# Last expert's down weights in four pieces by output columns, each added and normed as it comes; the final gain spread by TensorE

## The chip, the cores and the metric

The kernel runs on one core of one Trainium2 chip. The metric is the device time of one execution in microseconds (us). A core has TensorE (PE, matmuls, with its weight loads shown apart as PEld), VectorE (DVE), ScalarE (ACT), GpSimd (POOL) and SyncE (SP, which here issues nearly all DMAs). On-chip data lie in SBUF; matmul results lie in PSUM, which has eight banks of 128 partitions x 512 fp32 values.

## The reference

One decoder block on 256 tokens of width 1024, all in fp32: two attentions merged by gates, a residual, a hierarchical mixture of 32 experts, a second residual, and a last RMSNorm. What matters here is the end:

```python
def hier_moe(h, ...):
    ...                      # gates: (tokens, 32), two experts of one group per token
    out = jnp.zeros_like(hf)
    for e in range(N_EXPERTS):
        a = jax.nn.silu(hf @ w_e_gate[e]) * (hf @ w_e_up[e])     # 1024 -> 512
        out = out + gates[:, e:e + 1].astype(hf.dtype) * (a @ w_e_down[e])   # 512 -> 1024
    return out.reshape(b, t, d)
...
    x = x + hier_moe(rmsnorm(x, g_ffn[l]), ...)
return rmsnorm(x, g_final)
```

The last norm divides each token's row by the root of the mean of its squares and multiplies it by `g_final`, column by column.

## The kernel before

The 256 tokens are two tiles of 128 (NT = 2). The first 300 us, called the front here, are projections, the two attentions, the output projection and the routing; PE works nearly without a break there. Then comes the loop over 32 experts. Every expert has up to 32 slots (CAP) for its tokens. Its weights come in six chunks of 1 MB, four of gate/up and two of down, into a ring of 24 slots of SBUF, issued by SP in the order of use, with eight DMAs outstanding.

For each expert, `gateup` makes the activations (`gu`), `finish` transposes them (`atp`, copied to SBUF by DVE in L938) and multiplies them by the down weights. Here the width of 1024 is cut in four groups of 256 columns (REP = 4), and the four groups' matmuls fill four bands of 32 partitions of one bank `dn`. ACT and DVE then scale by the gate and split the result into a high and a low part, `y_hi` (L951) and `y_lo` (L953). `scatter_matrix` has made `ct`, a 0/1 matrix that spreads slots to tokens, and 16 matmuls per expert add both parts to the running sums, which stay in four PSUM banks `quad0` to `quad3` for the whole loop. Bank g holds columns 256g to 256g + 255 for both token tiles; the view is `yacc[g][:, t, :]`. The residual is added in the same banks. In the front the same four banks serve as work space: for transposes at the start, for the scores of the attentions (two banks per step, in turn) and for the router.

Small matmuls without use (`idle`, made by `busy`) stand between the chunks of the last two experts. The last expert's second down chunk comes in two DMAs of 512 KB, so that its last eight matmuls need only the last half. In the last expert the 16 matmuls into the banks go bank by bank. Behind it `norm` (L970 to L984) works through the sums, first token tile, then second: for each bank ACT squares it with a running sum (`zq`, L974), DVE multiplies it by the gain (`zo`, L975); then a reduce, a root (L271), a reciprocal (L272), a scaling of half the columns by each of ACT (L981) and DVE (L983), and two DMAs of 256 KB (L984). The gain `gf`, `g_final` broadcast to all partitions, comes by a DMA of 512 KB (L1086) behind the last weights, into a slot of the ring; `zq` and `zo` take two more slots. `general`, which follows, holds work for the case that an expert gets more tokens than slots; it is a branch that isn't taken.

Within an engine, instructions run in the order of the program. Waits between engines are semaphores, set from the tiles: an instruction waits for what touched its tile last on another engine. Two engines that read one PSUM tile also go one after the other: DVE's product on a bank waits for ACT's square on it.

Of the kernel before, what the change touches and what calls it, by code (L numbers as in the profile page):

```python
# [9 lines left out]
F32 = mybir.dt.float32  # L10
# [3 lines left out]
AF = mybir.ActivationFunctionType  # L14
ALU = mybir.AluOpType
AX = mybir.AxisListType

P = 128
T = 256
D = 1024  # L20
NT = T // P
NK = D // P
EPS = 1e-6
NE = 32
NG = 4
HID = 512
CAP = 32
REP = P // CAP
# [56 lines left out]
def tile_hybrid_block(  # L85
    ctx: ExitStack,
    tc: tile.TileContext,
    x, g_mix, w_in, w_kvs, sinks, w_br_dil, w_br_swa, w_out, g_ffn, w_group, b_group,
    w_router, b_router, w_e_gu, w_e_down, g_final, c_small, c_big, out,
):  # L90
    nc = tc.nc
    x, out = x[0], out[0]
# [7 lines left out]
    def slot(i, shape, name, dt=F32):  # L100
        return sb.tile(shape, dt, tag=f"s{i}", name=name)

    quad = [ps.tile([P, 512], F32, tag=f"quad{g}", name=f"quad{g}") for g in range(4)]

    def bank(tag, shape, name):
        return ps.tile(shape, F32, tag=tag, name=name)
# [537 lines left out]
    chunks = {}  # L644
    nchunk = [0]

    def fill(t, e, what, i):
        if what == 0:
            SP.dma_start(t, w_e_gu[e, i].rearrange("p u r c -> p (u r c)"))
        else:  # L650
            parts = 2 if (e, i) == (NE - 1, 1) else 1
            n = 2 // parts
            for j in range(parts):
                SP.dma_start(
                    t[:, 1024 * n * j:1024 * n * (j + 1)],
                    w_e_down[e, i, :, n * j:n * (j + 1), :].rearrange("p c o -> p (c o)"))

    def next_slot(name):
        nchunk[0] += 1
        return slot(ring[(nchunk[0] - 1) % len(ring)], [P, 2048], name)  # L660
# [272 lines left out]
    def finish(e):  # L933
# [28 lines left out]
               e == 0 and t == 0 and i == 0, e == NE - 1 and i == 1)  # L962
        yield

    cts = {}


# [3 lines left out]
    def norm(gf, zq, zo):  # L971
        for t in range(NT):
            for g in range(REP):
                A.activation(zq, yacc[g][:, t, :], AF.Square, accum_out=fs[:, t, g:g + 1])  # L974
                V.tensor_tensor(out=zo[:, t, g, :], in0=yacc[g][:, t, :], in1=gf[:, g, :], op=ALU.mult)  # L975
            V.tensor_reduce(fr[:, t:t + 1], fs[:, t, :], axis=AX.X, op=ALU.add)
            rstd_of(fr[:, t:t + 1], fr[:, t:t + 1])
            for h in range(2):
                z = zo[:, t, 2 * h:2 * h + 2, :]
                if h == 1:  # L980
                    A.activation(z, z, AF.Copy, scale=fr[:, t:t + 1])  # L981
                else:
                    V.tensor_scalar(z, z, fr[:, t:t + 1], None, op0=ALU.mult)  # L983
                SP.dma_start(out[t * P:(t + 1) * P, 512 * h:512 * h + 512], z.rearrange("p g c -> p (g c)"))  # L984

    def general(*tiles):

# [72 lines left out]
    for e in range(NE):  # L1060
# [14 lines left out]
        if e == NE - 1:  # L1075
            busy(e, 2)
        prefetch(4)
        fin = finish(e)
        cts[e] = scatter_matrix(e)
        run(fin)  # L1080
        run(gat)
        run(fin)
        prefetch(2)
        if e == NE - 2:
            gf = next_slot("gf")
            SP.dma_start(gf[:, 0:D], g_final.rearrange("(a d) -> a d", a=1).to_broadcast([P, D]))  # L1086
    run(fin)
    ordered[0] = False
    zq = next_slot("zq")[:, 0:256]
    zo = next_slot("zo").rearrange("p (t g c) -> p t g c", t=NT, g=REP)  # L1090
    tiles = (gf[:, 0:D].rearrange("p (g c) -> p g c", g=REP), zq, zo)
    norm(*tiles)
    general(*tiles)


_INS = ["x", "g_mix", "w_in", "w_kvs", "sinks", "w_br_dil", "w_br_swa", "w_out", "g_ffn", "w_group", "b_group",
        "w_router", "b_router", "w_e_gu", "w_e_down", "g_final"]


def _blocks(w):  # L1100
# [5 lines left out]
def _laid_out(inputs):  # L1106
# [8 lines left out]
        a[name] = _blocks(a[name][0])  # L1115
    gu = np.stack([a["w_e_gate"][0], a["w_e_up"][0]], axis=1)
    a["w_e_gu"] = gu.reshape(NE, 2, 4, 2, P, HID).transpose(0, 2, 4, 1, 3, 5)
    a["w_e_down"] = a["w_e_down"][0].reshape(NE, 2, 2, P, D).transpose(0, 1, 3, 2, 4)
    return a

# [26 lines left out]
```

## Time and profile before

| | |
|---|---|
| time, median of 3 runs | 750.15 us (749.88 to 750.56) |
| profiled execution | 749.57 us |
| its span, first to last instruction | 747.8 us |
| mean granted TensorE clock | 0.922 of full speed |
| busy: PE, DVE, ACT | 644.3, 297.0, 224.5 us |
| DMA, whole span | 249.87 MB, 334 GB/s |

Times in the rows are microseconds from the start of the span. A busy share is the share of a stretch in which an engine had an instruction in work; the chain of work is followed back from the last instruction, at each step to what released it. The granted clock is given as a share of 2.4 GHz, so that 0.50 is 1.2 GHz.

### The profile page before, as it was taken

The numbers are of one execution on the slowest core, as the hardware profiler recorded it, in microseconds if no ns is written. First come the engines' busy times: TensorE is split into PE (matmuls) and PEld (weight loads), VectorE is DVE, ScalarE is ACT, GpSimd is POOL, SyncE is SP. The second block draws the span as 40 slices with busy tenths as digits, with TensorE's granted clock in tenths as the row PEclk, the third lists the DMA queues.
The fourth block names the chain that finished last, engine by engine and source line by source line (L and its number), as shares of the span: only waits on it lengthen the run. The fifth ranks groups of instructions, "written<-read, shape, count | busy, mean of one in ns | idle before, by whom it ended". The sixth has DMA issues, their size and how long they took to land.

```text
span 747.8 us, 14858 instructions
## 1 busy us (share of the span) xinstructions
PE 644.3 (86%) x6416; PEld 459.5 (61%) x6416; DVE 297.0 (40%) x753; ACT 224.5 (30%) x448; POOL 2.1 (0%) x10
## 2 busy tenths in 40 slices
PE   9999999999999999999987687887678778777783
PEld 8999988888998998655544344344334434433341
DVE  6554767985788566532222112112111211111103
ACT  6444566775888443211101000001000000000004
POOL 0000000000000000000000000000000000000000
PEclk9999999999999999999999979789887978977887
DMA  8756446338837978999999999999999999999993
GB/s 323 270 188 223 142 142 223 114 114 293 327 114 293 348 272 288 369 388 419 419 418 420 419 420 420 419 419 422 420 419 422 418 420 421 420 420 420 420 417 123
DMA packets 39333, 249.87 MB, mean 334 GB/s; under 512 B 6608, under 2 KB 8032, under 8 KB 9824
## 3 DMA queue, kind: packets, MB, share of 16 engines
q1 hardware_dynamic: 39104, 248.81, 83.5%
q8 instruction: 52, 0.85, 0.5%
q10 hardware_dynamic: 160, 0.07, 0.1%
q14 instruction: 17, 0.14, 0.0%
HBM read 247.82 MB, written 1.05 MB: 333 GB/s over the span
## 4 chain that ended last, share of the span: by engine, by line
DMA 51%; PE 35%; DVE 7%; ACT 5%; issue 1%; SPq 0%; DVEq 0%; ACTq 0%
DMA ew<-in_w_e_gu_dram 30%; PE acc L119 23%; DMA ew<-in_w_e_down_dram 21%; PE gu L119 3%; DVE wh L244 3%; PE quad L119 2%; PE dn L119 1%; ACT wh L243 1%; ACT pps L500 1%; PE ga L119 1%; PE spun L119 1%; PE dpv L119 1%; PE dtp L580 1%; DVE kal L406 1%; DVE qs L396 1%
## 5 line engine op out<-in xcount | busy, mean ns | idle before, releaser
L119 PE MATMUL gu<-ew,xes 128*32 128x256 f32 x2048 | 153.7, 418 | 28.7 <-DMA ew<-in_w_e_gu_dram 28.5
L119 PE MATMUL acc<-hT_hi,wh 128*128 128x256 f32 x800 | 145.2, 283 | 0.8 <-DVE qa L396 0.8
L119 PEld LDWEIGHTS acc<-hT_hi,wh 128*128 128x128 f32 x800 | 121.6, 188 | 2.6 <-DVE qa L396 1.0
L119 PEld LDWEIGHTS gu<-ew,xes 128*32 128x32 f32 x2048 | 62.7, 117 | 88.6 <-DMA ew<-in_w_e_gu_dram 43.3
L244 DVE TENSOR_TENSOR wh<-w,wh 128x1024 fp32r<-128x1024 f32 (+1 forms) x84 | 100.2, 1198 | 35.0 <-ACT wh L243 33.1
L119 PE MATMUL acc<-hT_lo,wh 128*128 128x256 f32 x400 | 111.3, 279 | 0.0
L243 ACT CAST wh<-w 128x1024 fp32r<-128x1024 f32 (+1 forms) x84 | 86.2, 1028 | 41.4 <-PE acc L119 40.3
L119 PE MATMUL dn<-ew,ws 128*32 128x256 f32 x1024 | 82.9, 457 | 5.0 <-DMA ew<-in_w_e_down_dram 4.2
L925 DVE TENSOR_TENSOR ws<-ws,gu 128x128 f32<-128x128 f32 x32 | 9.2, 286 | 184.5 <-ACT ws L922 184.5
L119 PEld LDWEIGHTS acc<-hT_lo,wh 128*128 128x128 f32 x400 | 75.1, 188 | 0.0
L922 ACT ACTIVATE ws<-gu 128x128 f32<-128x128 f32 x32 | 8.9, 278 | 205.9 <-PE gu L119 205.9
L119 PEld LDWEIGHTS dn<-ew,ws 128*32 128x32 f32 x1024 | 32.2, 125 | 34.4 <-issue 10.7
L951 ACT ACTIVATE y_hi<-dn,gsl 128x256 fp32r<-128x256 f32 x32 | 15.2, 474 | 113.6 <-PE dn L119 113.6
L953 DVE SCALAR_TENSOR_TENSOR y_lo<-dn,gsl,y_hi 128x256 fp32r<-128x256 f32 x32 | 15.5, 484 | 67.9 <-ACT y_hi L951 67.9
L119 PE MATMUL ga<-ws,x_again 128*128 128x128 f32 x256 | 37.5, 307 | 4.8 <-DVE ws L938 3.8
L119 PEld LDWEIGHTS ga<-ws,x_again 128*128 128x128 f32 x256 | 34.2, 215 | 8.7 <-DVE ws L938 6.7
L119 PE MATMUL quad<-y_hi,cts 32*128 32x256 f32 x256 | 23.7, 355 | 15.0 <-ACT y_hi L951 15.0
L860 ACT ACTIVATE xes<-ga,fcol 128x128 f32<-128x128 f32 x32 | 11.6, 367 | 77.1 <-DVE xes L862 77.1
L119 PEld LDWEIGHTS quad<-y_hi,cts 32*128 32x128 f32 x256 | 13.9, 204 | 33.1 <-ACT y_hi L951 31.8
L119 PE MATMUL quad<-y_lo,cts 32*128 32x256 f32 x256 | 32.1, 386 | 2.4
L892 DVE TENSOR_SCALAR ws<-cs,pos 128x128 f32<-128x128 f32 x64 | 17.9, 282 | 40.4 <-PE ct L119 40.4
L119 PEld LDWEIGHTS quad<-y_lo,cts 32*128 32x128 f32 x256 | 18.6, 201 | 21.6 <-issue 13.9
(199 smaller groups left out, 737.0 us busy)
## 6 DMA issues: line engine op xcount, KB each, us to landing
ew<-in_w_e_gu_dram SPq DMA_DIRECT2D x128, 1024.0 KB, 19.8
ew<-in_w_e_down_dram SPq DMA_DIRECT2D x63, 1024.0 KB, 20.0
w<-in_w_in_dram SPq DMA_DIRECT2D x29, 1024.0 KB, 5.1
w<-in_w_br_swa_dram SPq DMA_DIRECT2D x4, 1024.0 KB, 5.3
w<-in_w_out_dram SPq DMA_DIRECT2D x4, 1024.0 KB, 5.1
w<-in_w_br_dil_dram SPq DMA_DIRECT2D x2, 1024.0 KB, 4.8
xt<-in_x_dram SPq DMA_DIRECT2D x2, 512.0 KB, 4.4
w<-in_w_in_dram SPq DMA_DIRECT2D x2, 512.0 KB, 6.4
```

The lines of the kernel that those rows point to most:

```text
L119: i = PE.matmul(o, lhsT, rhs, start=start, stop=stop, skip_group_check=True)
L243: order(A.copy(w[:, 0, :, :ncol], r))
L244: order(V.tensor_tensor(out=w[:, 1, :, :ncol], in0=r, in1=w[:, 0, :, :ncol].bitcast(F32), op=ALU.subtract))
L396: V.scalar_tensor_tensor(out=lo, in0=sv, scalar=cs[own, j:j + 1], in1=hi.bitcast(F32), op0=ALU.mult, op1=ALU.subtract)
L406: V.tensor_tensor(out=kal[r, b, c, :], in0=ov[own], in1=ka[own, b, c, :].bitcast(F32), op=ALU.subtract)
L500: A.activation(v, v, AF.Exp, bias=nm[:, i:i + 1], scale=-1.0, accum_out=den[:, i:i + 1])
L860: A.activation(dst, src, AF.Copy, scale=col)
L892: eq = V.tensor_scalar(dd[:, t, :].rearrange("p (g s) -> p g s", g=REP), cs[:, C_CNT:C_CNT + CAP].unsqueeze(1).to_broadcast([P, REP, CAP]) ...
L922: A.activation(ac, gu[:, 0:P], AF.Silu)
L925: V.tensor_tensor(out=ac, in0=ac, in1=gu[:, P:2 * P], op=ALU.mult)
L951: A.activation(y_hi, dn[:, 0:256], AF.Copy, scale=gsl)
L953: V.scalar_tensor_tensor(out=y_lo, in0=dn[:, 0:256], scalar=gsl, in1=y_hi.bitcast(F32), op0=ALU.mult, op1=ALU.subtract)
```

## The change

The four banks become one PSUM tile of four banks, `quads`, with `quad[g]` as views of it and a view `acc4` by token tile. The host lays out the last expert's down weights a second time, `w_e_last`, as four pieces; piece g holds, of each of the four groups of 256 columns, the columns 64g to 64g + 63, for all 512 inputs. They come in four DMAs of 512 KB in place of one of 1 MB and two of 512 KB.

The last expert has its own `finish_last`. For each piece in turn it does 16 down matmuls of 64 columns into a bank of its own, one scaling by the gate on DVE (`y`, plain fp32, no split), 8 plain fp32 matmuls that add 64 columns to each bank for both token tiles, and two squares on ACT, each over 64 columns in all four banks of one token tile. The products by the gain for piece g (`gained`) are written behind the `y` of piece g + 1. `norm_rest` then does the reduce, root and reciprocal once for both token tiles, the scalings (ACT 512 and 256 columns, DVE 512 and 768) and four output DMAs.

`g_final` comes as 4 KB in eight rows on ACT's queue at expert 2; at expert 29 `gains` spreads it over the partitions by eight matmuls and ACT copies it into the slot `gf`. The slots for `gf` and `zo` are taken at expert 28.

```diff
-    quad = [ps.tile([P, 512], F32, tag=f"quad{g}", name=f"quad{g}") for g in range(4)]
+    quads = ps.tile([P, 4, 512], F32, tag="quad", name="quad")
+    quad = [quads[:, g, :] for g in range(4)]
+    acc4 = quads.rearrange("p g (t c) -> p g t c", t=NT)
...
-            parts = 2 if (e, i) == (NE - 1, 1) else 1
-            n = 2 // parts
-            for j in range(parts):
-                SP.dma_start(
-                    t[:, 1024 * n * j:1024 * n * (j + 1)],
-                    w_e_down[e, i, :, n * j:n * (j + 1), :].rearrange("p c o -> p (c o)"))
+            if e == NE - 1:
+                for j in range(2):
+                    SP.dma_start(t[:, 1024 * j:1024 * j + 1024], w_e_last[2 * i + j].rearrange("p c j o -> p (c j o)"))
+            else:
+                SP.dma_start(t, w_e_down[e, i].rearrange("p c o -> p (c o)"))
...
+    def finish_last(e):
...
+        ct, gsl = cts.pop(e)
+        for g in range(REP):
+            dn = bank(("V", f"A{1 - e % 2}", "T", f"A{e % 2}")[g], [P, 512], f"dn{e}_{g}")
+            w = chunks[(e, 1, g // 2)][:, 1024 * (g % 2):1024 * (g % 2) + 1024].rearrange("p (c j o) -> p c j o", c=4, j=REP)
+            for c in range(4):
+                for j in range(REP):
+                    mm(dn[CAP * j:CAP * j + CAP, 0:64], aT[:, CAP * c:CAP * c + CAP], w[:, c, j, :], c == 0, c == 3)
+            y = sb.tile([P, 64], F32, tag=("yh", "yl")[g % 2], name=f"y{e}_{g}")
+            pin(V.tensor_scalar(y, dn[:, 0:64], gsl, None, op0=ALU.mult))
+            if g:
+                gained(g - 1)
+            for t in range(NT):
+                for j in range(REP):
+                    r = slice(CAP * j, CAP * j + CAP)
+                    mm(yacc[j][:, t, 64 * g:64 * g + 64], ct[r, t * P:(t + 1) * P].bitcast(F32), y[r, :], False, True)
+            for t in range(NT):
+                pin(A.activation(end["tiles"][1].rearrange("p (g c) -> p g c", g=REP), quarter(t, g), AF.Square,
+                                 accum_out=fs[:, t, g:g + 1]))
+        gained(REP - 1)
+        norm_rest()
...
+    def quarter(t, g):
+        return acc4[:, :, t, 64 * g:64 * g + 64]
+
+    def gained(g):
+        gf, zq, zo = end["tiles"]
+        for t in range(NT):
+            c = slice(64 * g, 64 * g + 64)
+            pin(V.tensor_tensor(out=zo[:, t, :, c], in0=quarter(t, g), in1=gf[:, :, c], op=ALU.mult))
+
+    def norm_rest():
+        gf, zq, zo = end["tiles"]
+        pin(V.tensor_reduce(fr, fs, axis=AX.X, op=ALU.add))
+        pin(A.activation(fr, fr, AF.Sqrt, scale=1.0 / D, bias=eps))
+        pin(V.reciprocal(fr, fr))
+        for t, k in ((0, 2), (1, 1)):
+            z = zo[:, t, 0:k, :]
+            pin(A.activation(z, z, AF.Copy, scale=fr[:, t:t + 1]))
+            SP.dma_start(out[t * P:(t + 1) * P, 0:256 * k], z.rearrange("p g c -> p (g c)"))
+            z = zo[:, t, k:, :]
+            pin(V.tensor_scalar(z, z, fr[:, t:t + 1], None, op0=ALU.mult))
+            SP.dma_start(out[t * P:(t + 1) * P, 256 * k:D], z.rearrange("p g c -> p (g c)"))
+
+    def gains():
...
+            for k in range(4):
+                mm(o[:, k * P:(k + 1) * P], ident[0:8, 4 * h + k:4 * h + k + 1].to_broadcast([8, P]), grows, True, True)
+            A.copy(gf[:, 2 * h:2 * h + 2, :], o.rearrange("p (g c) -> p g c", g=2))
...
-        if e == NE - 2:
+        if e == 2:
+            A.dma_start(grows, g_final.rearrange("(k p) -> k p", p=P))
+        if e == NE - 3:
+            gains()
+        if e == NE - 4:
             gf = next_slot("gf")
-            SP.dma_start(gf[:, 0:D], g_final.rearrange("(a d) -> a d", a=1).to_broadcast([P, D]))
+            zo = next_slot("zo").rearrange("p (t g c) -> p t g c", t=NT, g=REP)
```

On PE, the last expert before, from the transpose of its activations on (`atp`); `dn` are the down matmuls, `ew` the weight slots, `ws` the activations, `quad_61` to `quad_64` the four banks:

```order
L125 MATMUL atp_6646<-cs,ws 128x128
L119 MATMUL idle_6649<-y_hi_6562 128x256 x2
L119 MATMUL dn_6652<-ew_6291,ws 32x256 x8
L119 MATMUL dn_6652<-ew_6293,ws 32x256 x8
L119 MATMUL quad_61<-y_hi_6669,cts_6642 128x256 x2
L119 MATMUL quad_61<-y_lo_6670,cts_6642 128x256 x2
...
L119 MATMUL quad_64<-y_hi_6669,cts_6642 128x256 x2
L119 MATMUL quad_64<-y_lo_6670,cts_6642 128x256 x2
```

And the same place on PE after the change:

```order
L127 MATMUL atp_6657<-cs,ws 128x128
L121 MATMUL idle_6660<-y_hi_6575 128x256 x2
L121 MATMUL dn_0_6663<-ew_6289,ws 32x64 x16
L121 MATMUL quad<-y_0_6680,cts_6653 128x64 x8
L121 MATMUL dn_1_6692<-ew_6289,ws 32x64 x16
L121 MATMUL quad<-y_1_6709,cts_6653 128x64 x8
L121 MATMUL dn_2_6723<-ew_6292,ws 32x64 x16
L121 MATMUL quad<-y_2_6740,cts_6653 128x64 x8
L121 MATMUL dn_3_6754<-ew_6292,ws 32x64 x16
L121 MATMUL quad<-y_3_6771,cts_6653 128x64 x8
```

One round of 16 down matmuls and 16 adds has become four rounds of 16 narrow down matmuls and 8 narrow adds, with the down of a piece behind the add of the one before.

On DVE, from the copy of the transposed activations to the end, before:

```order
L938 COPY ws<-atp_6646 128x128
L953 SCALAR_TENSOR_TENSOR y_lo_6670<-dn_6652,gsl_6643,y_hi_6669 128x256
L975 TENSOR_TENSOR zo<-quad_61,gf 128x256
L975 TENSOR_TENSOR zo<-quad_62,gf 128x256
L975 TENSOR_TENSOR zo<-quad_63,gf 128x256
L975 TENSOR_TENSOR zo<-quad_64,gf 128x256
L976 TENSOR_REDUCE fr<-fs 128x1
...
L975 TENSOR_TENSOR zo<-quad_64,gf 128x256
L976 TENSOR_REDUCE fr<-fs 128x1
L272 RECIPROCAL fr<-fr 128x1
L983 TENSOR_SCALAR zo<-zo,fr 128x512
```

And after:

```order
L972 COPY ws<-atp_6657 128x128
L983 TENSOR_SCALAR y_0_6680<-dn_0_6663,gsl_6654 128x64
L983 TENSOR_SCALAR y_1_6709<-dn_1_6692,gsl_6654 128x64
L1026 TENSOR_TENSOR zo<-quad,gf 128x4x64 x2
L983 TENSOR_SCALAR y_2_6740<-dn_2_6723,gsl_6654 128x64
L1026 TENSOR_TENSOR zo<-quad,gf 128x4x64 x2
L983 TENSOR_SCALAR y_3_6771<-dn_3_6754,gsl_6654 128x64
L1026 TENSOR_TENSOR zo<-quad,gf 128x4x64 x4
L1030 TENSOR_REDUCE fr<-fs 128x2
L1032 RECIPROCAL fr<-fr 128x2
L1038 TENSOR_SCALAR zo<-zo,fr 128x512
L1038 TENSOR_SCALAR zo<-zo,fr 128x768
```

The products of a piece stand behind the `y` of the next one, each `L1026` reads all four banks, and the two norms, one for each token tile, have become one. On ACT the eight squares now stand in a row, ahead of one root and two scalings.

## Rows read from the trace of the kernel before

**Rows 1.** The cores view: span and mean granted clock.

```profile
core 0: 747.8 us, clock 0.922
```

**Rows 2.** The page: its chain's shares by engine, and its costliest group.

```profile
DMA 51%; PE 35%; DVE 7%; ACT 5%; issue 1%; SPq 0%; DVEq 0%; ACTq 0%
L119 PE MATMUL gu<-ew,xes 128*32 128x256 f32 x2048 | 153.7, 418 | 28.7 <-DMA ew<-in_w_e_gu_dram 28.5
```

**Rows 3.** Stretches: PE, PEld, DVE, ACT, POOL busy (instructions), granted clock, DMA share, GB/s.

```profile
700.00:723.30 23.30, 18.72 (x191) 9.14 (x186) 3.10 (x10) 1.50 (x4) 0.00 (x0) 0.78 1.01 420
723.30:727.00 3.70, 3.27 (x49) 1.79 (x38) 0.00 (x0) 0.00 (x0) 0.00 (x0) 1.00 1.01 415
...
734.60:737.00 2.40, 1.76 (x24) 1.02 (x24) 0.48 (x1) 0.57 (x2) 0.00 (x0) 0.98 0.06 24
737.00:743.00 6.00, 0.24 (x5) 0.00 (x0) 4.54 (x14) 5.40 (x20) 0.00 (x0) 0.50 0.15 51
```

**Rows 4.** Timeline, last expert: start, duration, engine, line, operation [idle before <-releaser].

```profile
732.18 0.62 PEld L119 LDWEIGHTS dn<-ew,ws 128*32 128x32 f32 x16 [0.41 <-DVE ws L938]
732.21 1.79 PE L119 MATMUL dn<-ew,ws 128*32 128x256 f32 x24 [0.23 <-DVE ws L938]
...
733.36 0.16 PEld L119 LDWEIGHTS dn<-ew,ws 128*32 128x32 f32 x8 [0.56 <-DMA ew<-in_w_e_down_dram]
734.62 0.64 PE L119 MATMUL dn<-ew,ws 128*32 128x256 f32 x8 [0.62 <-DMA ew<-in_w_e_down_dram]
```

**Rows 5.** The same timeline, the norm.

```profile
736.91 0.38 ACT L974 ACTIVATE zq<-quad 128x256 f32<-128x256 f32 x1 [1.11 <-PE quad L119]
...
737.41 0.38 ACT L974 ACTIVATE zq<-quad 128x256 f32<-128x256 f32 x1
737.41 1.95 DVE L975 TENSOR_TENSOR zo<-quad,gf 128x256 f32<-128x256 f32 x4 [1.10 <-ACT zq L974]
...
741.23 0.42 DVE L975 TENSOR_TENSOR zo<-quad,gf 128x256 f32<-128x256 f32 x1
...
741.56 0.15 DVE L976 TENSOR_REDUCE fr<-fs 128x1 f32<-128x4 f32 x1
...
742.27 0.49 DVE L983 TENSOR_SCALAR zo<-zo,fr 128x512 f32<-128x512 f32 x1
```

**Rows 6.** Tile gf (min/median/max ns, first and last start), then the output's line.

```profile
L975 DVE TENSOR_TENSOR zo<-quad,gf x8: 418/425/425, 737.4 to 741.2; 128x256 f32<-128x256 f32 x8
...
DMA to landing us min/median/max: 16.1/16.1/16.1
...
L984 SPq DMA_DIRECT2D out_dram<-zo x4: 332/379/678, 741.3 to 743.2; - x4
```

**Rows 7.** Timeline and clocks of narrow matmuls: eight, four and four, then sixteen.

```profile
297.92 1.08 PE L119 MATMUL quad<-wr,ws 128*128 128x36 f32 x8 [0.30 <-DVE ws L703]
...
702.21 0.50 PE L119 MATMUL ct<-gate,ws 128*128 128x1 f32 x4
...
717.55 0.85 PE L119 MATMUL ct<-gate,ws 128*128 128x1 f32 x4
...
702.00:703.00 1.00, 1.00 (x13) 0.81 (x17) 0.25 (x1) 0.00 (x0) 0.00 (x0) 0.89 1.02 426
717.50:718.50 1.00, 1.00 (x10) 0.98 (x12) 0.06 (x1) 0.00 (x0) 0.00 (x0) 0.50 1.00 418
...
723.72 0.39 PE L119 MATMUL quad<-y_hi,cts 32*128 32x256 f32 x4
...
724.18 0.28 PE L119 MATMUL quad<-y_lo,cts 32*128 32x256 f32 x4
```

**Rows 8.** Timeline of one place in attention: PE's scores and DVE's reads.

```profile
116.21 0.28 PE L119 MATMUL quad<-ka,qa 128*128 128x256 f32 x1
...
116.25 0.55 DVE L498 CUSTOM_DVE_ANT_0 pps<-quad,cb 128x384 f32<-128x384 f32 x1
...
116.77 0.68 PE L119 MATMUL quad<-qk 64*64 64x64 f32 x16
```

More of the change, by code (lines that the diff above doesn't have):

```diff
@@ L88, in tile_hybrid_block @@
     x, g_mix, w_in, w_kvs, sinks, w_br_dil, w_br_swa, w_out, g_ffn, w_group, b_group,
-    w_router, b_router, w_e_gu, w_e_down, g_final, c_small, c_big, out,
+    w_router, b_router, w_e_gu, w_e_down, w_e_last, g_final, c_small, c_big, out,
 ):
@@ L963, in finish @@
         yield
+    def finish_last(e):
+        ac = acts.pop(e)
+        tp = bank("T", [P, 512], f"atp{e}")
+        turn128(tp[:, 0:P], ac)
+        aT = ws[e % 2][:, 640:768]
+        V.tensor_copy(aT, tp[:, 0:P])
+        busy(e, 2)
+        yield
+        ct, gsl = cts.pop(e)
[18 more added lines that the diff above has]
+        norm_rest()
     cts = {}
@@ L984, in norm @@
                 SP.dma_start(out[t * P:(t + 1) * P, 512 * h:512 * h + 512], z.rearrange("p g c -> p (g c)"))
+    end = {}
+    def quarter(t, g):
[18 more added lines that the diff above has]
+    def gains():
+        gf, zq, zo = end["tiles"]
+        for h in range(2):
+            o = bank("TV"[h], [P, 512], f"gains{h}")
+            for k in range(4):
+                mm(o[:, k * P:(k + 1) * P], ident[0:8, 4 * h + k:4 * h + k + 1].to_broadcast([8, P]), grows, True, True)
+            A.copy(gf[:, 2 * h:2 * h + 2, :], o.rearrange("p (g c) -> p g c", g=2))
+    grows = late["ws"][0:8, 1536:1536 + P]
     def general(*tiles):
@@ L1077, in tile_hybrid_block @@
         prefetch(4)
-        fin = finish(e)
+        fin = (finish_last if e == NE - 1 else finish)(e)
         cts[e] = scatter_matrix(e)
@@ L1083, in tile_hybrid_block @@
         prefetch(2)
-        if e == NE - 2:
+        if e == 2:
[3 more added lines that the diff above has]
+        if e == NE - 4:
             gf = next_slot("gf")
-            SP.dma_start(gf[:, 0:D], g_final.rearrange("(a d) -> a d", a=1).to_broadcast([P, D]))
+            zo = next_slot("zo").rearrange("p (t g c) -> p t g c", t=NT, g=REP)
+            end["tiles"] = (gf[:, 0:D].rearrange("p (g c) -> p g c", g=REP), gf[:, D:D + 256], zo)
     run(fin)
     ordered[0] = False
[L1089 to L1093, printed above, removed]
+    general(*end["tiles"])
 _INS = ["x", "g_mix", "w_in", "w_kvs", "sinks", "w_br_dil", "w_br_swa", "w_out", "g_ffn", "w_group", "b_group",
-        "w_router", "b_router", "w_e_gu", "w_e_down", "g_final"]
+        "w_router", "b_router", "w_e_gu", "w_e_down", "w_e_last", "g_final"]
 def _blocks(w):
@@ L1117, in _laid_out @@
     a["w_e_gu"] = gu.reshape(NE, 2, 4, 2, P, HID).transpose(0, 2, 4, 1, 3, 5)
+    a["w_e_last"] = a["w_e_down"][0, NE - 1].reshape(4, P, 4, 4, 64).transpose(3, 1, 0, 2, 4)
     a["w_e_down"] = a["w_e_down"][0].reshape(NE, 2, 2, P, D).transpose(0, 1, 3, 2, 4)
```

## The prediction

> **What bounds the kernel now.** I read the cores view first: one core, span 747.8 us, mean granted clock 0.922 [rows 1]. The profiled execution took 749.57 us, 1.77 us more than its span, and is 0.58 us under the median of 750.15. Then the page's chain and the costliest groups: 51% of the span is DMA, and the gate/up matmuls alone sat idle 28.7 us, of which 28.5 for expert weights [rows 2]. So the expert phase runs at the speed of the weight stream, 420 GB/s with the DMA engines full until 727 us [rows 3]. Work added there on PE, ACT or DVE in small portions is hidden.
>
> The tail is not. In the timeline of the last expert the transposed activations are ready at 732.2 and three quarters of the down matmuls run at once or 1.2 us later; the last eight wait for the last half of a weight chunk until 734.62 [rows 4]. From there on it is a chain of engines [rows 5]: ACT and DVE make y, PE adds it to the four banks, and from 736.91 ACT squares and DVE products alternate, a bank apart: ACT starts one every 0.50 us, and the DVE product of a bank runs while ACT is on the next one. The last product starts at 741.23, the last scaling at 742.27, and the four output transfers are issued from 741.3 to 743.2 [rows 5, 6]. Two things are therefore to be compared after the change: the start of that last scaling, here called S (742.27 before), and what follows S.
>
> **The change, part by part.**
>
> *Weights by output columns.* The last expert's down weights are four pieces of 512 KB, the same bytes as one 1 MB and two 512 KB transfers. The halves of before became usable at 733.36 and 734.62, 1.26 us apart [rows 4], so the first piece should land near 734.6 - 3 x 1.26 = 730.8, before the activations are there (732.2). The first piece then starts at 732.2 and never waits for weights; the other three are in long before their turn. Gain: the chain starts 2.4 us earlier. That is all the change can win here, and it buys it by four rounds in place of one.
>
> *One round.* All of a piece's columns lie in all four banks (64 in each for either half of the tokens), and the four banks are now one tile. The order of PE is down, add, down, add; of DVE y, y, two products, y, two products, y, four products; and by the semaphores the add of piece g waits for both DVE products of piece g-1, the squares wait for the add, the products for both squares. Behind the waiting products on DVE stands only the y of the piece after next; behind the waiting add on PE the next piece's down. So add, squares, products is a closed loop, four times over. Prices at full clock:
> - down: 16 narrow matmuls. The 16 weight loads of before took 0.62 us and the last eight matmuls 0.64 with their end [rows 4]; 0.62 + 0.22 for the end = 0.84 until DVE starts.
> - y: 128x64 from PSUM on DVE, between the 0.15 of a 128x1 reduce [rows 5] and the 0.42 of a 128x256 product [rows 6]; a quarter of the way in elements: 0.22.
> - add: eight plain fp32 matmuls. Sixteen 32-row matmuls of another type took 723.72 to 724.46, 0.74 us; eight full-height fp32 ones took 1.08 [rows 7]. I take 0.74, since the rows are in four groups as there; ends 0.55 (sixteen 64x64 ones took 0.68 [rows 8], half of that and an end of 0.2) and 1.08.
> - squares: two of 128x256 elements, one start to the next 0.50 [rows 5]: 1.01.
> - products: two of 128x256 elements. One after the other start 0.33 apart (the last product at 741.23, the reduce behind it at 741.56 [rows 5]), one lasts 0.42 [rows 6]: 0.75. That the elements lie over four banks I take as costless.
> - three hand-overs between engines at about 0.03: 0.10.
>
> First add at 732.21 + 0.84 + 0.25 = 733.3, first square 734.05. A loop is 0.74 + 1.01 + 0.75 + 0.10 = 2.60, the next down and y lying beside the squares. Fourth pair of squares: 734.05 + 3 x 2.60 = 741.85; first of the last products 742.87. From the last product to the scaling it was 741.23 to 742.27, 1.04, and there is one product more, 0.33: S = 744.24, **+1.97** at full clock.
>
> *Clock.* The granted clock was 0.98 up to 737.0 and 0.50, the lower level of 1.2 GHz, from there on, where PE had next to nothing left to do [rows 3]. The new order leaves PE idle for most of every round, so I expect the lower level from the third piece on. Four narrow matmuls took 0.50 at 0.89 and 0.85 at 0.50 [rows 7]; part of each price is latency, so I put add at 1.10 and down at 1.25. Then y of pieces 2 and 3, which DVE has ahead of the products, come later than the squares end. Step by step: down of piece 2 from 736.5 to 737.65, y to 737.9, products 737.93 (0.3 late), add 738.7, squares 739.84; down of piece 3 from 739.7 to 740.95, y to 741.2, products 741.22 (0.35 late), add 742.0, squares 743.12, last products 744.13, S = 745.5: **+3.2**. With the clock as it was at 732 for all pieces it is the +1.97 above.
>
> *Norm and output.* The reduce, root and reciprocal now come once, in the same chain. Before, the first half's transfers were issued from 741.3 on, while the second half was still normed [rows 5, 6]; now all 1 MB goes after S. DVE has 512 and then 768 columns, 0.49 [rows 5] and 1.5 times that, so done at S + 1.2; an issue on SP takes 0.33 to 0.68 [rows 6], I take 0.45, so the four stand at S + 0.55, 1.0, 1.45, 1.9 in place of a last one at S + 0.94 (743.2). That is +0.9. The last transfer is 384 KB instead of 256 and has more in flight ahead of it; at the 420 GB/s of the weight stream [rows 3] 128 KB more is 0.3. Sum **+1.2**, between 0.9 and 1.6.
>
> *g_final.* The 512 KB broadcast landed 16.1 us after its issue, before anybody asked for it: the first product waited for ACT's square [rows 5, 6]. It goes; eight tiny matmuls and two copies come instead at expert 29, and a 4 KB transfer on ACT's queue at expert 2; they hide under the 28.5 us of waiting for weights [rows 2]. Two of the ring's slots go to the gains and the products at expert 28, when all weights are already issued. Zero; if the cover were gone, about 1.1 us for matmuls like those of [rows 7] and a copy.
>
> *One tile instead of four in the front.* Attention's scores and the start-up transposes use the same four banks. Where PE now wants another bank of the tile while DVE still reads one, it waits. In the trace only two of 16 score groups began before the reads of the slot ahead were over; in the one shown PE starts at 116.21 and DVE reads from 116.25 for 0.55 [rows 8], 0.6 us each, so 1.2 us at most, and PE bounds the front; a start-up conversion may come late by about as much. Other matmuls can stand in, so I take 0; ends 0 and +2.4.
>
> **By the notes.** That add, squares and products wait for each other is read above from the semaphores of the new program. The Trainium skill, page "PSUM — Partial Sum Buffer", section "PSUM bank collisions raise a hardware error", says that no two engines may be in one bank and the same quarter of its partitions at the same time, and that waits go by bank and not by address. With a piece in every bank this forbids overlap between neighbouring pieces in any version of this layout; in the trace of before ACT and DVE indeed keep a bank apart: the first product starts at 737.41, when ACT goes on to the second bank [rows 5]. By it the sum stays as it is, and the second rival below is excluded.
>
> **The sum.** 3.2 + 1.2 = +4.4: 749.57 + 4.4 = 754.0 for an execution like the profiled one, 754.6 with the 0.58 to the median.
>
> **Rivals.**
> 1. *The clock stays at its upper level.* Nothing else changes: +1.97 + 1.2 = +3.2, 753.3. For it: PE works again in every round, while before it had 0.24 us of work in six [rows 3]. Against it: one matmul group in 2.6 us. Chance 0.22.
> 2. *The rounds overlap.* If the adds did not have to wait for the products of the piece ahead, PE would set the pace with 0.84 + 0.74 = 1.58 a piece: fourth add ends at 732.2 + 4 x 1.58 + 0.25 = 738.8, squares to 739.8, S = 739.8 + 1.37 = 741.2, -1.1, and with the output +0.1: 750.3, no difference. This decides if a loop is under 1.6 us. Chance 0.10.
> 3. *Landing sets the pace.* The same overlap with down and add at 0.5 each, so that PE too is faster than 1.26 us a piece: last piece lands at 734.6, squares start at 735.85, end 736.85, S = 738.2, -4.1 + 1.2 = -2.9: 747.3. Against it: the full-height row of 1.08 and the waits. Chance 0.07.
> 4. *The front loses too*: +4.4 + 2.4 = 757.0 at the most, with one of the two pieces 755.8. For it: PE is the bound there; against: few groups came that early. Chance 0.11.
>
> **How the numbers follow.** The forecast, 754.6, has 0.50. Its own ends: add at 0.55 instead of 0.74 takes 3 x 0.2 = 0.6 off, and with output 0.9 and less lateness it is 753; add at 1.08 to 1.3 gives 755.8. The range leaves out rivals 2 and 3 and the top of 4, 0.2 in all: 751.5 to 757.0. What a measurement can tell from no change is about 0.2%, 1.5 us: faster by more is rival 3 and a little of 2, 0.08; within, most of 2 and a corner of 1, 0.13; slower, the rest, 0.79.
>
> **What would show it.** Right: in the timeline the first down of the last expert at 732.2 without a wait for weights; squares in four pairs about 2.6 us apart or more, each ended by a PE release, products behind them; PE's add waiting for DVE; S at 744 to 746; all output issues after S. Wrong: adds starting while DVE is still on the piece before (rival 2), PE waiting for weights between pieces (rival 3), clock 1.00 after 737 (rival 1), or a last expert that starts more than 1 us later than now (rival 4). A shorter pair of squares or a dn wait on the first piece would break single terms.

## The result: 756.7 us, 0.87% slower

The changed kernel takes 756.73 us (756.01 to 757.14), the kernel before 750.26 in the same comparison: a ratio of 1.0087, 95% interval 1.0074 to 1.0100. The direction was forecast and the time lies inside the range, near its upper end; the forecast was +4.4 us, measured were +6.5.

The profiled execution took 756.70 us with a span of 754.8, 7.0 more than [rows 1]; the one profiled before lay 0.7 under the median of its kernel, so that the spans differ by more than the medians. The clock as a mean is nearly the same:

```profile
core 0: 754.8 us, clock 0.920
```

Against [rows 2], the page of the changed kernel has PE where DMA was on part of the chain, while the gate/up matmuls waited about as long for weights in total. A sum over the phase doesn't show where the loss lies; the stretches below do:

```profile
PE 44%; DMA 43%; DVE 7%; ACT 4%; issue 1%; SPq 0%; ACTq 0%; DVEq 0%
L121 PE MATMUL gu<-ew,xes 128*32 128x256 f32 x2048 | 153.6, 418 | 27.9 <-DMA ew<-in_w_e_gu_dram 27.8
```

The timeline of the last expert and the norm (start, duration, engine, line, operation, idle before it and its releaser) answers [rows 4, 5]. `y` is at L983, the squares at L991 (`gf` stands as their output because the squared values, which nobody reads, go into an unused part of that slot), the products at L1026, the last scaling at L1038:

```profile
734.58 0.65 PE L121 MATMUL dn<-ew,ws 128*32 128x64 f32 x32
...
735.30 0.28 DVE L983 TENSOR_SCALAR y<-dn,gsl 128x64 f32<-128x64 f32 x1 [0.78 <-PE dn L121]
...
735.64 0.67 PE L121 MATMUL quad<-y,cts 32*128 32x64 f32 x16 [0.41 <-DVE y L983]
...
736.38 0.38 ACT L991 ACTIVATE gf<-quad 128x256 f32<-128x256 f32 x1 [1.38 <-PE quad L121]
...
737.39 0.76 DVE L1026 TENSOR_TENSOR zo<-quad,gf 128x256 f32<-128x256 f32 x2
...
738.20 0.67 PE L121 MATMUL quad<-y,cts 32*128 32x64 f32 x16 [1.31 <-DVE zo L1026]
...
738.99 0.38 ACT L991 ACTIVATE gf<-quad 128x256 f32<-128x256 f32 x1 [1.63 <-PE quad L121]
...
740.81 1.13 PE L121 MATMUL quad<-y,cts 32*128 32x64 f32 x16 [1.35 <-DVE zo L1026]
...
742.06 0.38 ACT L991 ACTIVATE gf<-quad 128x256 f32<-128x256 f32 x1 [2.09 <-PE quad L121]
...
745.27 0.38 ACT L991 ACTIVATE gf<-quad 128x256 f32<-128x256 f32 x1 [2.23 <-PE quad L121]
...
747.67 1.02 DVE L1038 TENSOR_SCALAR zo<-zo,fr 128x512 f32<-128x512 f32 x2
748.19 0.36 SPq L1039 DMA_DIRECT2D out_dram<-zo  x1
748.64 1.61 SPq L1036 DMA_DIRECT2D out_dram<-zo  x2
750.34 0.38 SPq L1039 DMA_DIRECT2D out_dram<-zo  x1
```

The reader is to see three things: the first down matmul starts without a wait for weights; each later add carries a wait for DVE's products (1.31, 1.35); and the squares start 2.61, 3.07 and 3.21 us apart. The scaling starts at 747.67 (S).

The whole difference of the two spans, 7.0 us, falls into five parts, cut at instructions that both kernels have:

| stretch | before | after | change | predicted |
|---|---|---|---|---|
| start to the weight issue at 306 us | 306.03 | 307.21 | +1.18 | 0 (ends 0 and 2.4) |
| from there to the last silu (730.76 and 733.21) | 424.73 | 426.00 | +1.27 | 0 (1.1 if uncovered) |
| last silu to the first down matmul | 1.45 | 1.37 | -0.08 | 0 |
| first down matmul to S | 10.06 | 13.09 | +3.03 | +3.2 |
| S to the end of the span | 5.52 | 7.16 | +1.64 | +1.2 |

### The profile page after: what moved, and what is told of

The parts are those of the page before. It is cut to its first block, busy times and chain, and to the rows that moved or that the text cites. A ratio compares the mean times of both kernels' runs of the same rounds, so it can differ in the third digit from the quotient of the medians.

```text
span 754.8 us, 15184 instructions
## 1 busy us (share of the span) xinstructions
PE 649.2 (86%) x6576; PEld 467.8 (62%) x6576; DVE 296.6 (39%) x754; ACT 225.1 (30%) x448; POOL 2.1 (0%) x10
## 3 DMA queue, kind: packets, MB, share of 16 engines
HBM read 247.30 MB, written 1.05 MB: 329 GB/s over the span
## 4 chain that ended last, share of the span: by engine, by line
PE 44%; DMA 43%; DVE 7%; ACT 4%; issue 1%; SPq 0%; ACTq 0%; DVEq 0%
DMA ew<-in_w_e_gu_dram 32%; PE acc L121 25%; DMA ew<-in_w_e_down_dram 11%; PE gu L121 6%; PE quad L121 4%; PE dn L121 2%; DVE wh L246 2%; PE ga L121 2%; ACT wh L245 1%; PE spv L121 1%; PE dpv L121 1%; PE dtp L582 1%; PE stp L544 1%; DVE kal L408 1%; DMA xt<-in_x_dram 1%
## 5 line engine op out<-in xcount | busy, mean ns | idle before, releaser
L121 PE MATMUL dn<-ew,ws 128*32 128x256 f32 (+1 forms) x1120 | 78.6, 414 | 5.1 <-DMA ew<-in_w_e_down_dram 4.5
```

What stands on the lines that cost most here:

```text
L121: i = PE.matmul(o, lhsT, rhs, start=start, stop=stop, skip_group_check=True)
```

## Experiments

### One tile alone

The kernel before, with one edit:

```diff
-    quad = [ps.tile([P, 512], F32, tag=f"quad{g}", name=f"quad{g}") for g in range(4)]
+    quads = ps.tile([P, 4, 512], F32, tag="quad", name="quad")
+    quad = [quads[:, g, :] for g in range(4)]
```

> The kernel before, with one edit: the four banks are one tile. In the changed kernel the first expert weights past the front were issued 1.2 us later than before and stayed 1.1 to 1.3 us late to the end. Theory (the shared tile makes start-up and attention wait): here too the weight issues after 300 us stand 1.0 to 1.4 us later than in the kernel before. The norm at the end, eight squares and eight products on one tile, can no longer overlap: each pair takes 0.50 + 0.42 and two hand-overs, about 1.0 instead of 0.50, so the end costs about 4 us more; together about +5 us, 755. Rival (the front moved because the scheduler had other instructions to place, the tile is innocent): weight issues within 0.3 us of before, total +4.

Measured: 754.14 us, ratio 1.0051 (1.0032 to 1.0071). The weight issue stands at 307.35, 1.32 later than in the kernel before. In the norm every square now waits for the product of the bank before it, where [rows 5] had one running beside the other:

```profile
739.21 0.42 DVE L976 TENSOR_TENSOR zo<-quad,gf 128x256 f32<-128x256 f32 x1 [1.43 <-ACT zq L975]
739.66 0.38 ACT L975 ACTIVATE zq<-quad 128x256 f32<-128x256 f32 x1 [0.49 <-DVE zo L976]
...
740.17 0.42 DVE L976 TENSOR_TENSOR zo<-quad,gf 128x256 f32<-128x256 f32 x1 [0.54 <-ACT zq L975]
740.63 0.38 ACT L975 ACTIVATE zq<-quad 128x256 f32<-128x256 f32 x1 [0.49 <-DVE zo L976]
```

A pair takes 0.97 us, as expected; from the first square (738.70) to S (747.01) 8.31 us instead of 5.36, so the end costs 3 and not 4. The tile was the only edit, so it is responsible for the later front and for the serial order.

How large is the front's part? The casts of the front's weights, matched one by one with those of the kernel before, say so. Between 40 and 281 us the six kernels with one tile lost 0.84, 0.99, 0.86, 0.91 and 0.84 us, and one 2.30; seven kernels with four tiles moved by -0.14 to +0.24. Up to 40 us the first lost 0.05 to 1.20 and the second -0.38 to +0.66, so the 0.34 at the start of the changed kernel are not told from scatter, though its trace has the wait (ACT at 14.34, 1.05 us for DVE's read of another bank):

```profile
14.34 0.47 ACT L307 ACTIVATE hT_hi<-quad,gcol 128x256 fp32r<-128x256 f32 x1 [1.05 <-DVE hT_lo L308]
```

A single weight issue isn't told from scatter either: in e12_later_fetch_14, with four tiles, it stood 2.00 late, in an execution with a granted clock of 0.66 from 300 to 305 us.

How the tile costs this in attention is open. PE does not sit idle for longer there: from 41 to 282 us it was busy for 235.96 to 236.16 us in the six kernels with one tile and for 235.01 to 235.28 in those with four. But the order of its matmuls in the front, the same in all kernels with four tiles, is another one in all six with one tile.

### Gains from memory again

In the changed kernel, the 4 KB transfer and `gains()` are taken out, and at expert 30:

```diff
+            SP.dma_start(gf[:, 0:D], g_final.rearrange("(a d) -> a d", a=1).to_broadcast([P, D]))
```

> The changed kernel, with the gains by the broadcast of 512 KB from memory again (issued behind the last weights), so without the eight matmuls and two copies at expert 29. In the changed kernel PE does not wait for weights from 699 us to the end, and the gain matmuls stand on the chain with 3.0 us; the last expert's first down matmul starts 2.4 us later than before, of which 1.2 comes from the front. Theory (the gain matmuls are the other 1.2): first down matmul about 1.2 us earlier than in the changed kernel, 733.4, total about 755.5. Rival (the low clock of that stretch made PE late, the matmuls only fell into it): no change, 756.7 within 0.5.

Measured: 758.20 us, ratio 1.0104 (1.0084 to 1.0123), outside both numbers. Two things came between. The front of this execution lost 2.68 us, 1.5 more than the changed kernel. That came between 159 and 171 us, where the granted clock of this execution fell (the 0.78 and 0.88 in these rows) and that of the changed kernel stayed at 1.00:

```profile
165.00:170.00 5.00, 3.60 (x20) 3.25 (x20) 2.86 (x7) 1.68 (x5) 0.00 (x0) 0.78 0.33 138
170.00:175.00 5.00, 5.00 (x49) 4.58 (x50) 2.81 (x8) 3.03 (x7) 0.00 (x0) 0.88 0.81 298
```

And the first products waited 1.2 us for the broadcast, which lands behind the last weights and is now wanted earlier than before:

```profile
DVE zo L1026 <- DMA gf<-in_g_final_dram: 1.2, 1, 1.2
```

What the run does tell: the last issue of gate/up weights (near 710 us) had moved by 2.89 against the kernel before, the last silu by 2.76. PE kept up with the weights. In the changed kernel the same two have moved by 1.18 and 2.44: PE fell 1.26 us behind. The time itself decides nothing between theory and rival.

### Unused matmuls in the rounds

```diff
+            if g:
+                for _ in range(8):
+                    mm(dn_ahead[:, 256:512], ct[:, 0:P], ct, True, True)
+            dn_ahead = dn
             y = sb.tile([P, 64], F32, ...)
```

> The changed kernel, with eight unused matmuls behind the down matmuls of pieces 1 to 3, into columns of a bank that nobody reads any more, so that PE is busy while it waits for the products. In the changed kernel the rounds took 2.61, 3.07 and 3.21 us, the clock falling at about 740.8. Theory (the longer rounds are the clock's doing): clock 1.00 to the last add, rounds of 2.6, the start of the scaling about 1.0 us earlier, total about 755.7. Rival (the longer rounds come from the waits between engines, or the clock falls anyway): rounds as before, total 756.7, or later by what the extra matmuls take, up to 757.5.

Measured: 755.46 us, ratio 1.0075 (1.0056 to 1.0094). Three windows of its stretches (PE, PEld, DVE, ACT, POOL busy, granted clock, DMA share, GB/s), first this kernel's rounds:

```profile
733.00:742.80 9.80, 8.55 (x217) 7.15 (x216) 3.50 (x11) 3.42 (x15) 0.00 (x0) 1.00 0.09 33
```

then the changed kernel's:

```profile
736.00:740.80 4.80, 2.15 (x92) 1.69 (x88) 2.08 (x6) 1.90 (x8) 0.00 (x0) 0.89 0.01 3
740.80:747.00 6.20, 3.27 (x64) 2.73 (x64) 1.66 (x6) 1.90 (x8) 0.00 (x0) 0.50 0.01 4
```

With PE kept busy the clock stayed at 2.4 GHz, all rounds took 2.61 us, and from the first down matmul to S it was 12.03 us in place of 13.09. The 1.06 us are the clock's, as the theory had it. The intervals of the two ratios overlap; it is the stretch that shows it.

### Pieces by bank

The same four transfers, now with the 256 columns of one bank each; four tiles again.

```diff
-                for j in range(REP):
-                    mm(dn[CAP * j:CAP * j + CAP, 0:64], aT[:, CAP * c:CAP * c + CAP], w[:, c, j, :], c == 0, c == 3)
+                mm(dns[g][CAP * c:CAP * c + CAP, 0:256], aT[:, CAP * c:CAP * c + CAP], w[:, c, :], True, True)
...
-                    mm(yacc[j][:, t, 64 * g:64 * g + 64], ct[r, t * P:(t + 1) * P].bitcast(F32), y[r, :], False, True)
+                mm(yacc[g][:, t, :], ct[:, t * P:(t + 1) * P].bitcast(F32), ys[g], False, True)
```

> The changed kernel with pieces cut by bank: piece g is the 256 columns of bank g, for all inputs; four down matmuls fill four bands of 32 rows with the partial sums of the four quarters of the inputs, and the add, over all 128 rows, sums them up. The four banks are four tiles again. Gains, one norm and the output are as in the changed kernel. Theory (the closed loop of add, squares and products is what a piece in all four banks costs): adds go on while ACT and DVE are on the bank before, only the last piece's chain remains behind the last weights, and the start of the scaling is near 739 to 740 with the front's 1.2 us back, 8 us earlier than 747.7; total 748.5 to 750. Rival (PE's order and prices set the pace, not the tie): rounds of about 1.6 us or more behind the start at 733.4, scaling at 742 or later, total 751 or more.

Measured: 752.45 us, ratio 1.0031 (1.0014 to 1.0048). The front is back (305.93), the waits of adds for products are gone, and yet S is 743.24, 9.95 us behind the first down matmul at 733.29. The rival had it: PE's own work fills the first round, add and down without a break, and most of the others:

```profile
734.54 1.13 PE L119 MATMUL quad<-y,cts 128*128 128x256 f32 x4 [0.17 <-DVE y L985]
735.60 0.64 PE L119 MATMUL dn<-ew,ws 128*32 128x256 f32 x8
736.17 1.13 PE L119 MATMUL quad<-y,cts 128*128 128x256 f32 x4
737.23 0.64 PE L119 MATMUL dn<-ew,ws 128*32 128x256 f32 x8
...
739.61 1.13 PE L119 MATMUL quad<-y,cts 128*128 128x256 f32 x4 [0.56 <-DVE y L985]
```

The first round takes 1.63 us, the next two 1.75 and 1.69; in the last of them the add waits for `y`, which stands on DVE behind the products of the bank before. So the round is 1.0 shorter than the closed loop's 2.6 at full clock. What the narrow pieces would take without the loop no run shows, since the matmuls are others: add 1.06 and down 0.57 here, 0.60 each in the changed kernel, from one start to the next. The last silu was 1.17 late, although the last weight issue had moved by 0.08 alone.

### The gains, with the front undisturbed

e4_by_bank, once with the gains from memory and once with the eight matmuls at expert 28 instead of 29.

> The pieces by bank (four tiles, as in e4_by_bank), with the gains by the broadcast of 512 KB behind the last weights instead of the eight matmuls. There the front stood 0.1 us earlier than in the kernel before, and yet the last expert's silu started 1.17 later. Theory (the gain matmuls at expert 29 make PE late, which cannot catch up before the end): silu at 730.8 to 731.0 as in the kernel before, the start of the scaling at 742.0 to 742.3, total about 751.2. Rival (it was the clock's phase): silu at 731.5 or later, total within 0.4 of 752.4.

> The pieces by bank, with the eight gain matmuls one expert earlier (28 in place of 29). Theory (PE works off the delay in its waits for weights, if there is an expert more for it): the last silu at 731.2 or earlier, total 751.2 to 751.8. Rival (PE never catches up in this stretch, or the matmuls are not the cause): silu at 731.9, total 752.4.

Measured: 751.72 us (ratio 1.0023, 1.0012 to 1.0035) with the last silu at 730.86, and 751.79 us (1.0027, 1.0014 to 1.0039) with the last silu at 730.70. Both silus as the theory had it; S was at 742.17 and 742.01, and the first total 0.5 higher than expected (its third output issue took 1.61 us; more on this below). The intervals of both ratios overlap with that of e4_by_bank, so the case rests on the silus. In the changed kernel's chain (start, duration, what) the matmuls stand with no wait for weights around them:

```profile
704.60 1.18 PE gains L121 x8
705.78 1.86 PE dn L121 x16
...
711.95 1.57 PE gains L121 x6
713.52 0.17 PE quad L121
713.69 0.26 PE gains L121 x2
```

From 690 us to the last expert PE waits for weights for 5.8 us in e6_bank_gf, 3.1 us in e4_by_bank and not at all in the changed kernel:

```profile
PE gu L119 <- DMA ew<-in_w_e_gu_dram: 5.8, 6, 1.4
```

So 3.0 us of PE went in at expert 29, and in these executions the slack left behind it was too small. One expert earlier it was enough. Over all profiles, PE's lateness (last silu less last weight issue, both against the kernel before) is -0.23 to +0.25 us in the eight kernels without matmuls at 29. In the five with them it is 1.26 (the changed kernel), 1.09 (e4_by_bank) and 1.26 (e9_no_general), but -0.05 and 0.00 in e3_busy_rounds and e5_out_even. Up to the last expert e3_busy_rounds, e5_out_even and e9_no_general differ from the changed kernel in no edit, and PE's matmuls come in the same order, so the difference lies between executions; the profiled ones of e3_busy_rounds and e5_out_even are 1.7 and 0.7 us under their kernels' medians. The matmuls at 29 thus made PE late in three executions of five, and what decides is open: the mean clock of 690 to 723 us (0.61, 0.73, 0.59 against 0.67 and 0.64) does not separate them.

### Even outputs

```diff
-        for t, k in ((0, 2), (1, 1)):
+        for t, k in ((0, 2), (1, 2)):
```

> The changed kernel, with its last scaling and output cut evenly: four transfers of 256 KB, ACT and DVE with 512 columns each for both token tiles, in place of 512, 512, 256 and 768. In the changed kernel the third issue on SP (the one of 256 columns) took 1.13 us in place of 0.36 to 0.38, so that the last stood at 2.67 us behind the start of the scaling and not at 1.9 as predicted. Theory (the narrow transfer, 1 KB a row, is what SP is slow to issue): all four issues under 0.5, last issue at 1.9, total 0.5 to 0.8 under the changed kernel's 756.7, 756.0. Rival (the third issue of a quick series is slow whatever its size): third issue over 0.8 again, no change beyond 0.3.

Measured: 756.58 us, ratio 1.0094 (1.0077 to 1.0111), and the third issue took 1.61 us, though it was as wide as the others. The width is not the cause; the last issue stood 3.15 behind S.

### Without the branch behind the norm

```diff
-    general(*end["tiles"])
```

> The changed kernel without the work for overfull experts and the branch over it (it leaves out that part, which is not taken with these inputs). In the traces of the changed kernel and of three others the third output issue on SP took 0.98 to 1.61 us and ended 0.3 to 0.4 after a 16 KB instruction fetch, which starts half a microsecond after PE has left its branch (3.4 us long) behind the last add; where the fetch came earlier the issue took 0.4. Theory (SP's issue stands still behind that fetch): without the branch no such fetch lies in the output, all four issues under 0.5, the last 1.9 behind the start of the scaling, total 0.6 to 1.5 under the changed kernel's 756.7. Rival (the third issue is slow for a reason of its own): 1.0 or more again, total within 0.4 of 756.7.

Measured: 755.84 us, ratio 1.0074 (1.0060 to 1.0089), with the last weight issue 2.21 late and PE another 1.26. The output itself is what the theory wanted: four issues of 0.35, 0.38, 0.40 and 0.40, the last 1.93 behind S, and S to the end of the span 5.49 in place of 7.16. Of these 1.67 us the issues make up 0.74 (1.93 in place of 2.67). The other 0.93 lie behind the last issue, 3.6 us to the end in place of 4.5 (4.6 in the kernel before); how much of them is the fetch and how much the branch that is gone is not shown. In the changed kernel PE's sequencer sits 3.4 us in the branch over that part (minimum, median and maximum in ns, start):

```profile
L1056 PEldq COMPARE_BRANCH  x1: 3402/3402/3402, 744.7 to 744.7; - x1
```

A first transfer of 16 KB on the instruction queue lies within the branch (745.75 to 746.68). PE leaves it at 748.1, and another runs from 748.85 to 749.98. SP's third issue begins at 749.11 and ends at 750.24. The queues of that stretch, 748.5 to 750.3 (packets, MB, share of 16 engines), have it:

```profile
q8 instruction: 1, 0.02, 3.9%
```

and those of the kernel without the branch have no such line between 748.5 and 752. The same pair stands in four other traces: fetch ends at 749.28, 744.87, 744.06, and, in the kernel before, 742.11, the issue under way at 749.64, 745.22, 744.44 and 742.48 (there the second, with 0.68). It stands in e2_gf_dma and e4_by_bank too, where the third issue took 1.88 and 1.26. Where the fetch was over before (e3_busy_rounds) the issue took 0.4, and an issue that began before the fetch was not held (the second of the changed kernel, 0.38). The Trainium skill, page "Runtime: NRT & Kernel Launch", section "Instruction fetch mechanics", says that a taken branch whose target isn't in an engine's current window of instructions forces a fetch by DMA; the trace agrees, with PE 3.4 us in its branch and a fetch in that time. That SP's issue stands behind that fetch is shown here by the times and by the run without the branch.

### A version built from this

By bank, gains from memory, `y` in two parts so that the adds are single-pass, DVE ahead with `y`, bank 3 multiplied by its gain in the last scaling:

```diff
-            pin(V.tensor_scalar(ys[g], dns[g][:, 0:256], gsl, None, op0=ALU.mult))
+            pin(V.scalar_tensor_tensor(out=lo[g], in0=dns[g][:, 0:256], scalar=gsl, in1=hi[g].bitcast(F32),
+                                       op0=ALU.mult, op1=ALU.subtract))
...
+            pin(V.scalar_tensor_tensor(out=zo[:, t, 3, :], in0=yacc[3][:, t, :], scalar=fr[:, t:t + 1],
+                                       in1=gf[:, 3, :], op0=ALU.mult, op1=ALU.mult))
```

> The pieces by bank with the gains from memory, and three edits from the rows of e4_by_bank, where a round took 1.63 us of PE (down 0.57, add 1.06): y in two parts again, so that the adds are single-pass matmuls (0.11 a piece's matmul instead of 0.27); DVE makes y ahead of the products, and bank 3 gets its gain in the last scaling; output in four even transfers, one of them issued by ACT. Theory (PE's rounds were the bound there): a round under 1.26, so the landing of the last piece at 734.6 sets the end, start of the scaling at 738.5 to 739.5, total 748 to 749, faster than the kernel before. Rival (ACT's squares or DVE's parts of y take PE's place, 1.5 to 1.7 a round): scaling at 740.5 to 742, total 749.5 to 751, no gain.

> e8_bank_v2 with all four output transfers issued by SP. There the scaling started at 739.5, 2.8 earlier than in the kernel before, but the last data landed at 745.8, as in the kernel before (745.7): the last packets of one DMA engine came 1.5 us behind the others, when an instruction fetch of 1.51 us stood among them. Theory (the fetch and the write of 1 MB in one go set the end, not the queue): the same end within 0.4, total 749.7 to 750.5. Rival (two queues at once cost it): total 748.5 to 749.5, faster than the kernel before.

Measured: 750.09 us, ratio 1.0000 (0.9991 to 1.0010), and 749.71 us, ratio 1.0002 (0.9993 to 1.0011). S is at 739.51 and 739.76, 2.8 and 2.5 us earlier than before, inside or next to the theory's range, and nothing of it reaches the end: S to the end is 8.2 us in place of 5.5. The first total misses its theory's 748 to 749, the second is what its theory said. The whole output now leaves behind S, in one go. In 40 slices of 735 to 748 (e8_bank_v2):

```profile
GB/s 0 0 0 0 0 0 0 0 25 0 50 0 0 0 0 0 0 0 50 391 384 403 353 366 353 366 372 151 38 25 25 25 25 0 0 0 0 0 0 0
```

Most is through in nine slices, 2.9 us, eight of them at 350 to 400 GB/s; then comes a trickle of 25 GB/s for 1.5 us, about the share of one of 16 DMA engines (400 over 16). A fetch of 1.51 us (from 741.97) ran among the data. The second kernel, with all issues on SP, has the same end, so two queues at once are not the cause. Two more moved the fetch by unused matmuls on PE behind the last add:

```diff
+        for _ in range(28):
+            mm(dns[0][:, 256:512], ct[:, 0:P], ct, True, True)
```

> e10_bank_v2_sp with 28 unused matmuls on PE behind its last add, so that PE comes to its branch about 3 us later and the 16 KB instruction fetch behind it (742.15 for 1.56 us there, in the middle of the output) starts at about 745, behind the output's data. Theory (the fetch holds up one DMA engine's share of the output: data to 746.0, though 1 MB at 370 GB/s from 741.4 is through at 744.2): last data at 744.3 to 744.8, total 748.3 to 749.0, faster than the kernel before. Rival (the last packets are late for another reason): last data at 745.8 or later, total 749.5 to 750.5.

> The same with 14 unused matmuls: the fetch about 1.5 us later, at about 743.7, where the output's data still run. Theory: last data still late, 745.5 or more, total 749.3 to 750.2, between e10_bank_v2_sp and e11_late_fetch. Rival (the fetch is innocent): no difference to e11_late_fetch.

Measured: 750.47 us (ratio 1.0003, 0.9994 to 1.0012) and 750.09 us (0.9995, 0.9986 to 1.0005), no gain, the last data at 747.2 and 747.9. S stood at 740.45 and 741.97 in these executions, so that the last data came 6.8 and 5.9 us behind it, 6.3 in the two kernels above. The theory's numbers are missed, without a clean answer: there are two fetches, one in PE's branch and one behind it, and neither edit moved both out of the output. With 28 matmuls the first fell on the second issue (0.87) and the other into the data (744.57 to 746.21); with 14 the other fell on the fourth issue (1.40), and the third took 0.81 beside an 8 KB fetch on another instruction queue (743.57 to 744.32).

The kernel that has no fetch in its output is e9_no_general, and its 1 MB, all behind S too, has no trickle. In 40 slices of 748.5 to 753.5:

```profile
GB/s 0 0 0 0 0 0 0 0 0 0 0 0 164 442 344 377 377 426 328 344 426 410 377 320 336 319 484 410 393 393 393 393 393 393 148 0 0 0 0 0
```

It is through in 2.9 us, and S to the end is 5.49, no more than with the staggered output of before. This speaks for the fetch, and what else hangs on the branch, as what ate the gain. It is not shown, for the pieces by bank without the branch were not run. If S to the end were 5.5 there too, a span of about 745 would follow from S at 739.5, an estimate.

## Why the prediction was right, and where it was short

The time lies inside the range and the mechanism of the rounds is the one forecast, but two stretches that had been taken as zero cost 1.2 and 1.3 us. By the prediction's own signs, the squares in four pairs, the adds that wait for DVE and the issues behind S came; the first down at 732.2 and S at 744 to 746 did not (734.58 and 747.67), and the last expert started 2.4 us later, which was its sign of rival 4. That the range held is in part luck: its upper end allowed 2.4 us for the front, of which the front took 1.2 and the gains, for which nothing was allowed, 1.3 in the profiled execution.

- **The rounds: right.** Predicted +3.2, measured +3.03; at full clock +1.97 predicted, and with busy rounds 12.03 less 10.06, the same. The closed loop was 2.60 predicted, 2.61 measured for a round at full clock. Down was 0.72 to `y` (0.84 predicted), `y` 0.34 to the add with its hand-over (0.25), add 0.74 in the first round and 0.79 in the next (0.74), two squares 1.01, two products 0.81 with their hand-over (0.75 without).
- **The clock: right, one down later.** It fell between the third down and the third add, about 739.7 (a mean of 0.89 from 736 to 740.8 and 0.50 behind it), where the forecast had the third down slow already. The slow prices were add 1.25 (1.10 predicted) and down 1.15 (1.25). These errors partly cancel; the share of the clock, 1.06 measured by the busy rounds, was 1.2 predicted.
- **Output: mis-sized by 0.4, from two errors that partly cancel.** The step that failed is "an issue on SP takes 0.33 to 0.68, I take 0.45": the third took 1.13 behind the fetch, and the last stood 2.67 behind S. Without the fetch it was 1.93, 1.9 predicted. The 0.3 for the last transfer's data did not come: from the last issue to the end it was 4.5 us, 4.6 before.
- **g_final: taken as zero, cost 1.3 where PE came late.** The step "they hide under the 28.5 us of waiting for weights" took a sum over 32 experts for the cover at expert 29. [rows 3] already showed PE busy 18.72 of 23.3 us near the end, at a mean clock of 0.78. The price of 1.1 us was too low as well: it was 3.0, 1.18 for the first half, mostly at a granted clock of 1.00, and 1.83 for the second at 0.50.
- **The front: taken as zero, cost 1.2.** Rival 4 had it, with 0.11. The step that failed is "Other matmuls can stand in, so I take 0": the one tile cost 0.84 to 0.99 in attention in five of the six kernels (2.30 in the sixth, with the clock's fall), between the two ends given. That PE waits for banks there, as the forecast's upper end had it, is not shown; what the traces show is another order of its matmuls.
- **Rivals 2 and 3** would have needed more than the tie's removal: by bank, without a tie, S was still 9.95 behind the first down. That its first round of 1.63 us is near rival 2's 1.58 is chance, for its matmuls are others. With the front and the gains out of the way (e6_bank_gf) S is at 742.17, where rival 2 had 741.2, and the time 751.7.

## What to carry to other kernels

The semaphores go by tile: two engines that read different banks of one PSUM tile wait for each other here, and the norm took 8.3 us in place of 5.4. A tile made larger for one instruction at the end touches everything that used its banks before, here 0.9 us in attention, 240 us long. Cover has to be counted where the work is put: waits summed over a phase say nothing about the last experts, where PE at the lower clock had almost none left, and in three executions of five it came late. And an earlier last computation is worth only what its output lets through: 2.8 us at the scaling became zero when all of 1 MB was written behind it with an instruction fetch among the data, while the same 1 MB without the branch and its fetch took no longer behind S than a staggered output.

## What the hardware showed that was not expected

An instruction fetch of 16 KB behind PE's branch held up the DMA issue on another engine's queue, SP: an issue that began during the fetch took 0.68 to 1.88 us in place of 0.33 to 0.40, ending 0.3 to 0.4 behind the fetch, in nine traces. And with eight unused matmuls a round the granted clock stayed at 2.4 GHz to the last add, worth 1.06 us, where with PE waiting it fell to 1.2 GHz.
